# A recurrence spread over the projections of a hybrid decoder layer: later and held products, its end moved over the output projection, and norms regrouped

## The chip, the cores and the metric

The kernel runs on one core of a Trainium2 chip. A core has a matmul engine (TensorE, PE in the profile; PEld is its weight load), VectorE (DVE), ScalarE (ACT), GpSimd (POOL) and SyncE (SP), each with a queue of its own that it works off strictly in order, and 16 DMA engines that serve transfers asked for by SP's and POOL's queues. The metric is the device time of one launch in microseconds; the time of a kernel is the median of its runs.

## The reference

One layer of a decoder, on 512 prompt tokens and on 8 sampled sequences of 4 tokens. Everything is float32, width 2048.

```python
h = rms_norm(x, norm_mix_w)
proj = h @ w_in                      # [B_a|C_a|h_a|q|k|v|z: 1024 each | a: 8 | b: 8]
y_a = b_a * dwconv3(c_a * h_a)       # then RMSNorm over each group of 128
q, k, v = silu(dwconv4(q|k|v))       # q, k L2-normalised per head (8 heads of 128)
g = -exp(a_log) * softplus(a + dt_bias);  beta = sigmoid(b)
# gated delta rule, per head:
#   S_t = alpha_t S_{t-1} (I - beta_t k_t k_t^T) + beta_t v_t k_t^T ;  o_t = S_t q_t
o = rms_norm(o, dn_norm_w) * silu(z)
x = x + concat(y_a, o) @ w_out       # 2048 x 2048
h = rms_norm(x, norm_ffn_w)
x = x + square(relu(h @ w_up)) @ w_down     # 2048 -> 8192 -> 2048
return rms_norm(x, final_norm_w), new conv states, new S
```

The delta rule is evaluated in chunks: in each chunk a unit lower triangular system is inverted (here a substitution over 32 rows and then block products), and the state S passes from chunk to chunk.

## The kernel before

**Layout.** Activations lie transposed: 128 features on the partitions, tokens along the free axis. The 512 prompt tokens and 32 sampled ones make two halves of `HT` = 272 columns. A product of float32 accuracy is made of three products of rounded parts: `product` (L146) multiplies high weight by high activation, high by low, and low by high, for both halves, so one 128x128 block of weights costs six matmuls of 272 columns. `weight` loads up to 1024 columns of weights on SP's queue (L118) into one of two `w_raw` buffers, ScalarE rounds them (`w_hi`, L119), VectorE takes the rest (`w_lo`, L122); there are three buffers of each. `ahead` asks for weights two items early. `split` (L130, L131) does the same to an activation tile; 32 buffers of the pool `hl` hold the parts, all of them in use during the input projection.

**The mixer.** The input projection has 56 slabs of 128 output columns, in four groups (`gi`) of two heads: six slabs of q, k and v, six of the convolution path (C, h, B twice), two of z. The first three slabs of all run together while `x` arrives tile by tile; in that stretch ScalarE also squares the tiles and GpSimd and VectorE add them up (`ssq`), and the row norm follows (`rstd_rows`: products with ones at L153, then Ln and Exp on ScalarE at L156 and L157, then VectorE from L158). Each further slab has 16 blocks, 96 matmuls; after every second block the code calls `run_side`. I call the twelve matmuls between two calls a **share**; a slab is eight shares.

**Side work.** `run_side` advances a list of Python generators: `yield n` means "go on n shares later". Per group there are four kinds. `decays` loads and exponentiates the decay rows; it waits until the recurrence before is done. `delta` is the prompt's recurrence, appended after the sixth slab, so that 64 shares of its group are left: transposes and norms of k (L506), the in-chunk products (L532), a round trip through DRAM and the substitution of 31 steps on VectorE (L557, L561), another round trip (tiles `ti`, `tn`), transposes of v, then `yield W_SUBST`; then block products of 32x32 and 64x64 (L595, L607, L612, L618, L624), four chunks in which the state is passed on (L638, L644, L652, L662, L663), and the norm of the output per head (sums over features by L681, L682, then Ln and Exp at L685, L686), multiplied by `silu(z)` and written to the DRAM tile `cat`. `delta_sample` does the same for the sampled tokens (state products L738, four iterations L747, new states L782). `norm` closes a convolution slab (L472 to L479).

**Who sets the order.** Each engine's order is not the order of the code. A planner runs through the program with a cost model before the launch: it hands each engine, at each moment, the instruction of highest priority whose inputs it reckons ready. Priority is the place in the code, raised by `urgent` or `high_priority`. So an instruction whose inputs the planner reckons late is placed late, and everything behind it in its chain is then overdue and placed as soon as it is reckoned ready. On the chip that order is fixed, and an engine waits at an instruction whose input is really later. `keep_in_program_order` ties an instruction behind the one that stands before it in the code on its engine.

**After the mixer.** `run_side(True)` finishes what is left; then the sixteen tiles of `cat` are loaded and split (L866), the mixer's pools are closed, and tiles of new pools take the same memory, so their loads wait for the old tiles' last use: the residual `x2p` (eight tiles, L889, pool `g`), and later more. The output projection runs in two parts: first (`w_o1`) 16 output blocks over eight tiles of `cat`, added into `x2p` (L898), then (`w_o2`) the other eight, by halves, with squares for the second row norm. The up projection follows: three plain blocks, then `Pair`s that need seven block products instead of eight (`bilinear`, L1093) and load four quarter weights `w_q` each (L1043) and combine them on VectorE (L1053 to L1056), four tiles at a time in pool `g`. The down projection runs in visits of the same kind, from a new pool of six, with eight `Plain` items (L146, six us of products each) set between the first visits; it reads tiles `uc` back from DRAM. The last part adds the remaining terms, makes the third row norm and writes the output.

**Activation tables.** ScalarE needs a table that holds the function it is to compute. `ln_exp` loads one set that holds both Ln and Exp; where it isn't called, a load is placed before each function that the current set lacks (`ACT_TABLE_LOAD`, shown at the line of the function). The load at `ln_exp` has L79, that of Silu L84.

## Time and profile before

| | |
|---|---|
| Median of 3 runs | 2474.48 us (2472.3 to 2479.77) |
| The profiled execution's own time | 2472.83 us |
| Its span, first to last instruction | 2471.1 us |
| Mean granted TensorE clock | 0.986 |
| Instructions | 47391, of them 19089 matmuls |
| Moved by DMA | 398 MB, mean 161 GB/s |

The stages in the profiled execution: input projection from the first microseconds to 837, first part of the output projection to about 945, second part to about 1047, up projection to about 1740, down projection to about 2400, last part to 2455 on TensorE, and then row norm and output. In the profile's rows "a<-b,c" means that tile a is written from b and c, xN counts instructions, and a bracket at the end of a row gives the idle time of the engine before it and what ended it. Matmuls are pipelined and their ends are modelled, so starts are a better measure of TensorE's pace than busy time.

### The profile page before, as it was taken

The numbers are of one execution on the slowest core, as the hardware profiler recorded it, in microseconds if no ns is written. First come the engines' busy times: TensorE is split into PE (matmuls) and PEld (weight loads), VectorE is DVE, ScalarE is ACT, GpSimd is POOL, SyncE is SP. The second block draws the span as 40 slices with busy tenths as digits, with TensorE's granted clock in tenths as the row PEclk, the third lists the DMA queues.
The fourth block names the chain that finished last, engine by engine and source line by source line (L and its number), as shares of the span: only waits on it lengthen the run. The fifth ranks groups of instructions, "written<-read, shape, count | busy, mean of one in ns | idle before, by whom it ended". The sixth has DMA issues, their size and how long they took to land.

```text
span 2471.1 us, 47391 instructions
## 1 busy us (share of the span) xinstructions
PE 2407.6 (97%) x19089; PEld 2375.8 (96%) x19089; DVE 1803.2 (73%) x2939; ACT 1095.5 (44%) x1611; POOL 494.7 (20%) x776
## 2 busy tenths in 40 slices
PE   8999999999999999999999999999899999999997
PEld 7999999999999899898999999999899999999996
DVE  8776576567567635787888888888478877888885
ACT  5425334332531523565555555555233333333445
POOL 5124114213312303410111111101401212121003
PEclk9999999999998999999999999999999999999998
DMA  6233233332422535556555555556945656464433
GB/s 199 84 117 119 88 107 116 95 104 89 128 89 90 197 112 191 193 193 225 198 197 193 184 185 191 196 193 214 372 144 166 224 164 224 154 222 155 127 98 103
DMA packets 144276, 397.96 MB, mean 161 GB/s; under 512 B 35349, under 2 KB 44217, under 8 KB 144057
## 3 DMA queue, kind: packets, MB, share of 16 engines
q1 hardware_dynamic: 108648, 266.12, 34.2%
q0 software_dynamic: 35408, 128.82, 13.9%
q8 instruction: 150, 2.46, 0.4%
q14 instruction: 70, 0.57, 0.1%
HBM read 317.37 MB, written 77.49 MB: 160 GB/s over the span
## 4 chain that ended last, share of the span: by engine, by line
PE 80%; DVE 8%; DMA 7%; ACT 3%; issue 2%; SPq 0%; POOL 0%; DVEq 0%; ACTq 0%; POOLq 0%
PE ps_s L1093 45%; PE ps_big L146 27%; DVE w_lo L122 2%; PE ps_sm L146 2%; DMA w_raw<-in_w_up_dram 2%; DMA w_raw<-in_w_o_dram 2%; DMA w_q<-in_w_d_dram 2%; PE ps_s L146 1%; ACT w_hi L119 1%; DVE w_lo L1061 1%; PE ps_sm L738 1%; DVE x L937 0%; DVE x2v L1250 0%; PE ps_sm L532 0%; DMA tn<-ti 0%
## 5 line engine op out<-in xcount | busy, mean ns | idle before, releaser
L1060 ACT ACTIVATE w_hi<-w_q 128x768 fp32r<-128x768 f32 (+3 forms) x422 | 375.3, 889 | 554.5 <-PE ps_s L1093 461.4
L1093 PE MATMUL ps_s<-uc,w_hi 128*128 128x272 f32 x3136 | 594.6, 289 | 7.9 <-DVE x2v L898 3.9
L1093 PEld LDWEIGHTS ps_s<-uc,w_hi 128*128 128x128 f32 x3136 | 492.5, 189 | 11.7 <-ACT w_hi L1060 6.8
L1061 DVE TENSOR_TENSOR w_lo<-w_q,w_hi 128x768 fp32r<-128x768 f32 (+3 forms) x422 | 424.8, 1008 | 63.0 <-ACT w_hi L1060 61.4
L1093 PE MATMUL ps_s<-uc,w_lo 128*128 128x272 f32 x1568 | 451.5, 288 | 4.5 <-DVE w_lo L1061 4.5
L146 PE MATMUL ps_big<-x_hi,w_hi 128*128 128x272 f32 x1984 | 423.3, 293 | 1.5 <-ACT x_hi L134 1.5
L146 PE MATMUL ps_big<-x_hi,w_lo 128*128 128x272 f32 x1984 | 418.2, 291 | 2.6 <-DVE w_lo L122 2.6
L146 PE MATMUL ps_big<-x_lo,w_hi 128*128 128x272 f32 x1984 | 418.9, 292 | 0.3 <-DVE x_lo L137 0.3
L119 ACT ACTIVATE w_hi<-w_raw 128x1024 fp32r<-128x1024 f32 (+3 forms) x215 | 211.2, 982 | 406.0 <-PE ps_big L146 250.8
L122 DVE TENSOR_TENSOR w_lo<-w_raw,w_hi 128x1024 fp32r<-128x1024 f32 (+3 forms) x215 | 275.1, 1280 | 149.0 <-ACT w_hi L119 144.8
L146 PEld LDWEIGHTS ps_big<-x_hi,w_hi 128*128 128x128 f32 x1984 | 315.5, 189 | 5.4 <-ACT x_hi L134 2.2
L146 PEld LDWEIGHTS ps_big<-x_hi,w_lo 128*128 128x128 f32 x1984 | 314.5, 190 | 4.1 <-DVE w_lo L122 3.3
L146 PEld LDWEIGHTS ps_big<-x_lo,w_hi 128*128 128x128 f32 x1984 | 314.3, 190 | 1.0 <-DVE x_lo L137 0.5
L1093 PEld LDWEIGHTS ps_s<-uc,w_lo 128*128 128x128 f32 x1568 | 296.0, 189 | 4.9 <-DVE w_lo L1061 4.9
L1093 PE MATMUL ps_s<-c_hi,w_lo 128*128 128x272 f32 x928 | 267.7, 288 | 2.5 <-DVE w_lo L122 1.4
L1093 PE MATMUL ps_s<-c_hi,w_hi 128*128 128x272 f32 x928 | 266.5, 287 | 2.6 <-ACT w_hi L1060 2.2
L1093 PE MATMUL ps_s<-c_lo,w_hi 128*128 128x272 f32 x928 | 266.4, 287 | 0.0
L1160 POOL DMA_DIRECT2D uc<-ucd x196 | 106.5, 548 | 438.4 <-PE ps_s L1093 385.9
L898 DVE TENSOR_TENSOR x2v<-x2v,ps_s 128x272 f32<-128x272 f32 x326 | 139.8, 433 | 68.0 <-PE ps_s L1093 57.4
L1093 PEld LDWEIGHTS ps_s<-c_hi,w_lo 128*128 128x128 f32 x928 | 174.4, 188 | 3.5 <-DVE w_lo L122 1.8
L1093 PEld LDWEIGHTS ps_s<-c_hi,w_hi 128*128 128x128 f32 x928 | 174.6, 188 | 3.0 <-ACT w_hi L1060 2.4
L1093 PEld LDWEIGHTS ps_s<-c_lo,w_hi 128*128 128x128 f32 x928 | 174.4, 188 | 0.0
(378 smaller groups left out, 4304.5 us busy)
## 6 DMA issues: line engine op xcount, KB each, us to landing
w_q<-in_w_up_dram SPq DMA_DIRECT2D x116, 512.0 KB, 5.3
w_raw<-in_w_in_dram SPq DMA_DIRECT2D x106, 512.0 KB, 3.4
uc<-ucd POOLq DMA_DIRECT2D x196, 272.0 KB, 6.0
w_q<-in_w_d_dram SPq DMA_DIRECT2D x128, 384.0 KB, 3.3
w_raw<-in_w_o_dram SPq DMA_DIRECT2D x32, 512.0 KB, 3.5
ucd<-u_hi POOLq DMA_DIRECT2D x28, 544.0 KB, 5.7
ucd<-tc POOLq DMA_DIRECT2D x28, 544.0 KB, 6.9
w_raw<-in_w_up_dram SPq DMA_DIRECT2D x28, 512.0 KB, 3.6
```

The source lines that it names most:

```text
L119: S.activation(hi[:, c], raw[:, c], AF.Copy)
L122: V.tensor_tensor(lo[:, c], raw[:, c], hi[:, c].bitcast(F32), SUB)
L146: PE.matmul(ps[h], wp[:, c : c + P], x, start=start and i == 0, stop=stop and i == 2)
L738: PE.matmul(prq[rows, :], flat[:, 64 * b : 64 * b + 64], s0[:, b, :], start=b == 0, stop=b == NB - 1,)
L898: V.tensor_tensor(out, out, ps, ADD)
L1060: S.activation(hi, s, AF.Copy)
L1061: V.tensor_tensor(lo, s, hi.bitcast(F32), SUB)
L1093: PE.matmul(ps, wp[:, k * P : (k + 1) * P], xp, start=p in (1, 2, 5) and k == j == 0, stop=k == len(c) - 1 and j == 2, skip_group_check=True,)
L1160: nc.gpsimd.dma_start(t.bitcast(F32), uc_d[KS[j]][:, 2 * b : 2 * b + 2])
```

## The change

1. `W_SUBST` goes from 17 to 32, and three more `yield 1` stand between the halves of the block products; the sample path waits 13 shares instead of 2 before its iterations and 4 instead of 3 after them.
2. TensorE is called through a class `PE`: the first product or transpose of each side step is tied behind the product before it in the code.
3. After the last slab, twelve tiles of `cat` are loaded (four of them into a new pool `xe` of two buffers, early), the first two residual tiles take the same two buffers, and the first four blocks of the output projection run with `run_side` between them; only then is the side work drained and the rest of `cat` loaded. All sixteen blocks use the double accumulators.
4. The output norms of a group's two heads run side by side in tiles that reuse the recurrence's, with one table load; the products with `silu(z)` go to tiles of their own.
5. `ln_exp(True)` is called after the output projection's first part, ahead of the later row norms.
6. At the start, the last two tiles of `x` are squared before the last weights are asked for.
7. Pool `g` has six buffers instead of eight; each fourth tile of that kind comes from `xe`.
8. Five `Plain` items instead of three run before the first visit of the down projection, one (not two) after it, one (not two) after the second.

```diff
-W_SUBST = 17
+W_SUBST = 32
+N_MIX = 4
...
+    class PE:
+        step = False
+        @classmethod
+        def held(cls, ins):
+            if cls.step:
+                tc.keep_in_program_order(ins)
+                cls.step = False
+            return ins
+        @classmethod
+        def matmul(cls, *args, **kw):
+            return cls.held(nc.tensor.matmul(*args, **kw))
...
+    xep = pool("xe", 2)
...
+            if kp == KT // 2 - 1:
+                square_of(0)
+                square_of(1)
             w = weight(a["w_first"][kp], 2 * N_START * P, None if kp else first)
...
                 V.tensor_copy(x1[hi_], px[hi_])
+                yield 1
...
-            yield 2
+            yield 1
...
                 V.tensor_scalar(tt[lo_, :, hi_], py[lo_], -1.0, None, MUL)
+                if p2 == 0:
+                    yield 1
...
+            nk, nf = tile_in(dp, "nk", [P, 2, 2, L], tag="at"), tile_in(dp, "nf", [P, 2, L], F32R, tag="vs")
+            nl = tile_in(dp, "nl", [P, 2, L], F32R, tag="ke")
             for hl in range(2):
...
-                yield 5
-                pn = ps_small()
...
-                ln_exp(True)
...
+            yield 5
+            ln_exp(True)
+            for hl in range(2):
+                sk, pn = nk[:, 1, hl], ps_small()
+                PE.matmul(pn, ones_r, nf[:, hl], start=True, stop=False)
+                PE.matmul(pn, ones_r, nl[:, hl], start=False, stop=True)
...
+            while not z_done[gi]:
+                yield 3
+            for hl in range(2):
+                o = tmp()[:, :L].rearrange("p (a c) -> p a c", a=2)
+                G.tensor_tensor(o, og[:, hl, :, :HP], nk[:, 1, hl].rearrange("p (a c) -> p a c", a=2), MUL)
                 nc.gpsimd.dma_start(cat_d[8 + 2 * gi + hl][:, :, :HP], o)
...
-            yield 2
+            yield 13
             y = rq
...
-            yield 3
+            yield 4
...
                     try:
+                        PE.step = True
                         item[0] = next(item[1]) - 1
...
+            PE.step = False
...
+        cat = []
+        for n, i in enumerate(W_OUT_ORDER[:12]):
+            if n < 4:
+                if n % 2 == 0:
+                    pair = tile_in(xep, "cat2", [P, 2, 2, HT], tag="xe")
+                yr = pair[:, n % 2]
+            else:
+                yr = tmp2()
+            with tc.high_priority(offset=WPRIO if n < 4 else 0):
+                nc.sync.dma_start(yr, cat_d[i])
+            cat.append(split(yr, None))
+        x2p = [tile_in(xep, f"x2_{i}", [P, 2, 2, HT], tag="xe") for i in range(2)]
+        for i in range(2):
+            with urgent():
+                nc.sync.dma_start(x2p[i], a["x"][i])
...
+        def first_part(last, between):
+            for (ob, q), w in firsts:
+                if q == 0:
+                    first_part.ps = ps_big()
+                ps = first_part.ps
+                for k in range(N1 // 2):
+                    kk = N1 // 2 * q + k
+                    product(ps[0], w, k * P, cat[kk], kk == 0, kk == N1 - 1)
+                    if k % 2:
+                        between()
+                if q == 1:
+                    add(x2p[ob // 2][:, ob % 2], ps[1])
+                if (ob, q) == (last, 1):
+                    return
+
+        first_part(N_MIX - 1, run_side)
         run_side(True)
-        cat = []
-        for i in W_OUT_ORDER:
+        for i in W_OUT_ORDER[12:]:
             yr = tmp2()
             nc.sync.dma_start(yr, cat_d[i])
             cat.append(split(yr, None))
...
-    gp = pool("g", 8)
+    gp = pool("g", 6)
...
+    def gx_tile(i, name, shape):
+        return tile_in(xep, name, shape, tag="xe") if i % 4 == 3 else g_tile(name, shape)
...
-        if q == 0:
-            ps = ([ps_small(HT) for _ in range(2)], None) if ob in (2, 3) else ps_big()
...
+    first_part(KT - 1, lambda: None)
+    ln_exp(True)
...
-    items[0] = plains[:3] + items[0] + plains[3:5]
-    items[1] += plains[5:7]
+    items[0] = plains[:5] + items[0] + plains[5:6]
+    items[1] += plains[6:7]
     items[2] += plains[7:]
```

More of the change, by code (lines that the diff above doesn't have):

```diff
@@ L861, in trunk, with add @@
         assert next(jobs, None) is None
+        cat = []
[4 more added lines that the diff above has]
+                yr = pair[:, n % 2]
+            else:
+                yr = tmp2()
[4 more added lines that the diff above has]
+        for i in range(2):
+            with urgent():
+                nc.sync.dma_start(x2p[i], a["x"][i])
+        def add(out, ps):
+            with urgent():
+                V.tensor_tensor(out, out, ps, ADD)
+        firsts = ahead([(o, q) for o in range(KT) for q in range(2)],
+                       lambda it: weight(a["w_o1"][2 * it[0] + it[1]], N1 // 2 * P))
+        def first_part(last, between):
[13 more added lines that the diff above has]
+        first_part(N_MIX - 1, run_side)
         run_side(True)
-        cat = []
-        for i in W_OUT_ORDER:
+        for i in W_OUT_ORDER[12:]:
             yr = tmp2()
@@ L884, in c_tile @@
         return tile_in(p, name, [P, 2, HT], F32R, tag="hl" if p is hlp else "c")
-    x2p = [g_tile(f"x2_{i}", [P, 2, 2, HT]) for i in range(KT // 2)]
-    for i in range(KT // 2):
+    for i in range(2, KT // 2):
+        x2p.append(g_tile(f"x2_{i}", [P, 2, 2, HT]))
         with tc.high_priority(offset=WPRIO if i < 5 else 0):
@@ L894, in trunk @@
     uc_d = {m: tile_in(dram, f"ucd{m}", [P, 14, HT]) for m in range(N_PLAIN, NF - 1)}
-    def add(out, ps):
-        with urgent():
-            V.tensor_tensor(out, out, ps, ADD)
-    ps = None
-    for (ob, q), w in ahead([(o, q) for o in range(KT) for q in range(2)],
-                            lambda it: weight(a["w_o1"][2 * it[0] + it[1]], N1 // 2 * P)):
-        if q == 0:
-            ps = ([ps_small(HT) for _ in range(2)], None) if ob in (2, 3) else ps_big()
-        for k in range(N1 // 2):
-            kk = N1 // 2 * q + k
-            product(ps[0], w, k * P, cat[kk], kk == 0, kk == N1 - 1)
-        if q == 1 and ps[1] is not None:
-            add(x2[ob], ps[1])
-        elif q == 1:
-            for h in range(2):
-                add(x2[ob][:, h], ps[0][h])
+    first_part(KT - 1, lambda: None)
+    ln_exp(True)
     early.close()
@@ L1040, in load @@
                 with urgent():
-                    self.q = [self.tile(self.n) for _ in range(4)]
+                    self.q = [self.tile(self.n, i) for i in range(4)]
                     for t, s in zip(self.q, self.src):
@@ L1116, in residual @@
         for i in r:
[L1117 removed]
+            x2v.append(gx_tile(i, f"x2v{i}", [P, 2, 2, HT]))
             queue.dma_start(x2v[i], x2_d[i])
```

55 lines of the change are left out of this document (24 added, 31 removed).

## The prediction

> **What bounds the kernel now.** I read the page first: engine totals and the chain that ended last.
>
> ```profile
> span 2471.1 us, 47391 instructions
> PE 2407.6 (97%) x19089; PEld 2375.8 (96%) x19089; DVE 1803.2 (73%) x2939; ACT 1095.5 (44%) x1611; POOL 494.7 (20%) x776
> PE 80%; DVE 8%; DMA 7%; ACT 3%; issue 2%; SPq 0%; POOL 0%; DVEq 0%; ACTq 0%; POOLq 0%
> ```
>
> TensorE sets the time, so an edit is worth the TensorE time it gives back. A busy PE says little here, since a matmul that crawls at half clock also counts as busy. I therefore count matmul starts per stretch. Windows view: length, busy time with starts (x) of PE, PEld, DVE, ACT, POOL, then granted clock, DMA share, GB/s.
>
> ```profile
> 240.00:290.00 50.00, 50.00 (x401) 50.00 (x400) 28.76 (x37) 14.18 (x23) 13.20 (x30) 1.00 0.30 93
> 178.00:210.00 32.00, 30.70 (x304) 28.16 (x303) 21.87 (x66) 8.58 (x19) 11.00 (x12) 1.00 0.18 57
> 376.00:408.00 32.00, 30.10 (x276) 27.50 (x276) 19.39 (x61) 5.57 (x14) 6.86 (x8) 0.89 0.22 63
> 578.00:610.00 32.00, 30.86 (x283) 28.27 (x281) 19.71 (x61) 5.93 (x14) 6.92 (x9) 0.89 0.22 64
> 780.00:820.00 40.00, 38.11 (x309) 35.42 (x308) 23.38 (x66) 9.23 (x20) 10.58 (x12) 0.79 0.12 32
> 855.00:868.00 13.00, 8.47 (x52) 8.26 (x51) 4.13 (x7) 2.52 (x4) 0.00 (x0) 0.74 0.92 348
> 1760.00:1772.00 12.00, 4.79 (x23) 3.44 (x21) 4.79 (x14) 1.97 (x5) 6.66 (x13) 0.72 1.04 385
> 1055.00:1066.00 11.00, 9.00 (x59) 8.78 (x59) 8.26 (x16) 8.43 (x12) 0.36 (x1) 0.84 0.29 97
> 38.00:47.00 9.00, 5.96 (x32) 5.33 (x31) 7.00 (x13) 2.89 (x5) 0.41 (x1) 0.81 0.88 250
> 2429.00:2446.00 17.00, 16.03 (x122) 15.23 (x121) 12.20 (x21) 10.21 (x20) 6.18 (x7) 1.00 0.36 126
> ```
>
> The first row is the undisturbed pace: 401 starts in 50 us, **0.125 us** a 272-column product. By it the handover to the output projection (855 to 868) lost 13 - 52 x 0.125 = 6.5 us, the start of the down projection (1760 to 1772) 12 - 23 x 0.125 = 9.1, the second row norm (1055) 3.6, the first (38) 5.0, the one at 2429 1.8. The four recurrences (rows 2 to 5) need the small products priced apart. The same view of the slab products alone, then two stretches of group 3:
>
> ```profile
> 178.00:210.00 32.00, 18.75 (x109) 14.75 (x108) 1.00 0.18 57
> 376.00:408.00 32.00, 17.99 (x91) 13.93 (x90) 0.89 0.22 63
> 578.00:610.00 32.00, 18.22 (x95) 14.22 (x93) 0.89 0.22 64
> 780.00:820.00 40.00, 23.47 (x114) 18.97 (x113) 0.79 0.12 32
> 707.20:783.45 76.25, 68.25 (x524) 66.35 (x524) 1.00 0.36 109
> 783.45:816.10 32.65, 17.94 (x72) 13.77 (x72) 0.74 0.08 24
> ```
>
> And from the chain of waits (start, us, what) and PE's timeline, one row each for the price of a small product and for what starts a recurrence:
>
> ```profile
> 741.69 1.89 PE ps_sm L738 x16
> 778.59 4.21 DMA tn<-ti
> 789.55 1.90 PE ps_sm L618 x16
> ```
> ```profile
> 706.37 1.03 PE L506 MATMUL ps_sm<-ident,kq 128*128 128x128 f32 x8
> 783.49 0.69 PE L595 MATMUL ps_sm<-tn,at 32*32 32x32 f32 x16 [1.02 <-DVE tn L575]
> ```
>
> A full-size small product costs 1.89 / 16 = 0.118 us; a 64x64 one 0.119 at half clock, so 0.06; a 32x32 one 0.043. The code issues 80 of 32x32 and 32 of 64x64 per recurrence (eight products are sixteen instructions, as the L595 row shows). Group 3: 114 x 0.125 + 80 x 0.043 + 32 x 0.06 + 83 x 0.118 = 29.4 of 40 us, **lost 10.6**. Groups 0, 1, 2 the same way: 3.2, 6.7, 5.8. Sum 26.3 us. Granted clock explains 0.11 x 32 twice and 0.21 x 40, that is 15.4 of it.
>
> Why they lose is an order, visible in two counts. The code asks for L595 31 shares (of twelve products) after L506: 4 + 8 + 2 + 17. The trace has 524 / 12 = 43.7 shares between. So the planner found the substitution's answer (the tn transfer, row 778.59) later than asked; after that every step of the recurrence is overdue and goes out as soon as the planner believes it ready, with 72 slab products between L595 and 816 instead of the 19 shares (228) that its yields ask for. TensorE sees the whole chain of replies nearly bare.
>
> **The change, part by part.**
>
> *Substitution 17 to 32 shares, products held, three more yields.* L595 is now asked for 46 shares after L506, 2.3 shares (3.5 us) past where it stood; its wait was 1.02 us, so it finds its operand. Then 17 steps follow, each behind at least twelve products, 1.5 us. The reply that a step needs is a VectorE copy, at worst behind one weight split:
>
> ```profile
> 800.25 1.22 DVE L122 TENSOR_TENSOR w_lo<-w_raw,w_hi 128x1024 fp32r<-128x1024 f32 x1
> 801.38 0.48 DVE L646 COPY y<-ps_sm 128x128 f32<-128x128 f32 x2
> ```
>
> 1.7 us at worst, 0.48 at best, against 1.5 plus the step's own products (four at 0.118). Most steps are covered, and they now fall into the two z slabs, whose VectorE job is a single product. I take 22 of the 26.3 back; bounds 10 (0.25 us left on each of 68 steps) and 26. The held instruction blocks what is behind it on PE, slab products above all; that is what a wrong cover would cost, priced below. Recurrence and sample path now end five to seven shares into the next group's q slab, beside its decays and convolutions: VectorE stood at 28.76 of 50 us there, so I charge 1 us, 0 to 6.
>
> *Last group over four output blocks.* In the trace the handover loses like this (SP's queue, then PE's):
>
> ```profile
> 852.36 2.36 SPq L889 DMA_DIRECT2D x<-in_x_dram  x5
> 854.83 0.93 SPq L118 DMA_DIRECT2D w_raw<-in_w_o_dram  x2
> ```
> ```profile
> 863.26 0.82 PE L146 MATMUL ps_sm<-x_hi,w_hi 128*128 128x272 f32 x2 [4.53 <-ACT w_hi L119]
> ```
> ```profile
> x<-in_x_dram SPq DMA_DIRECT2D x8, 544.0 KB, 5.9
> w_raw<-in_w_o_dram SPq DMA_DIRECT2D x11, 256.0 KB, 3.3
> ```
>
> Five residual loads of 544 KB go out ahead of two weights, all in one burst; at 348 GB/s they take 8 us, and PE runs dry. After the change two residual tiles and four `cat` tiles have their own buffers and load earlier, and three urgent loads are left for the burst: about 5 us. But those wait for the mixer's memory, and the mixer now ends later: norms 10 shares (15 us) past the last slab, then ACT, VectorE and two POOL products, say 22 us. The fifth block needs its residual at 5 x 48 x 0.125 = 30 us and a second accumulator lends 6 more, so a 5.9 us load fits. Behind the waiting loads in SP's queue stand the `w_o1` weights, and TensorE waits for those. I take 4 of the 6.5; bounds -6 and 6.5.
>
> *One table for the norms.* ScalarE at the tail, and VectorE's two waits there (line, total, times, longest):
>
> ```profile
> 2455.49 1.28 ACT L156 ACT_TABLE_LOAD   x1
> 2456.79 0.49 ACT L156 ACTIVATE r<-ps_sm,eps_t 128x272 f32<-128x272 f32 x1
> 2457.30 1.28 ACT L157 ACT_TABLE_LOAD   x1
> 2458.59 0.43 ACT L157 ACTIVATE r<-r 128x272 f32<-128x272 f32 x1
> ```
> ```profile
> DVE rt L158 <- ACT r L157: 9.4, 2, 4.7
> ```
> ```profile
> DVE rt L158 <- ACT r L157: 5.2, 2, 2.6
> ```
>
> Both loads at the tail lie on the way to the end, nothing covers them: 2.56, less 0.3 for the result of the last row sum. At 999 and 1056 (last row) VectorE, which splits the weights, stands 2.6 us behind the same pair; freeing it gives about 3 of the 3.6 us lost at 1055 and 1 at 1000; 0.7 of the 1.8 at 2429. Term 7, bounds 3 (tail alone) and 10. It rests on Ln and Exp staying loaded through the Relus between, which no row shows. The Trainium skill (ScalarE: Activation LUTs, "Table sets: the hidden batching unit") lists relu and copy as filler of every set, which speaks for it. Its section "What ACT_TABLE_LOAD costs" puts a switch at about 2.66 us with a drain; here Ln starts 0.02 us after a 1.28 us load, so the trace disagrees; by the page the term would be about 14.
>
> *Plain products first.* The 9.1 us at 1760 (rows: who waits on SP, then the chain):
>
> ```profile
> SPq L1043 <- DMA ud<-u: 15.1, 1, 15.1
> ```
> ```profile
> 1756.33 11.12 DMA w_q<-in_w_d_dram
> ```
>
> The first quarter weights wait for memory of a tile on its way out, then 11.12 us in a saturated window (share 1.04), until 1767.5. Two more plain items are 2 x 48 x 0.125 = 12 us of work that needs none of this, and PE reaches the first visit at about 1773. Their two 512 KB weights go ahead (2.7 us at 385 GB/s), and later visits have one plain item less between them. Term 8, bounds 2 (a plain weight stuck behind the six waiting loads on SP) and 10.
>
> *Squares first at the start.* PE stood 5.0 us at 38 for the row sum, but VectorE has no gap before it; the same splits come 1.4 us later. Term 1, -1 to 4. *Six plus two g tiles*: the first quarters now wait for the fifth residual tile to be freed, not the fourth; -1, -3 to 0. *Row norms side by side, own output tiles, renamed tags*: the same ACT, VectorE and POOL operations on engines at 73% and below, nothing.
>
> **Sum**: 22 - 1 + 4 + 7 + 8 + 1 - 1 = 40 us. The profiled execution took 2472.8 (span 2471.1 plus 1.7), so 2432.8; it was 1.7 below the median of the runs, so **2434.5 us**.
>
> **The rivals.**
>
> *The clock stays low.* If the small products themselves pull the granted clock down, and not the bare replies between them, closing the waits doesn't bring it back and the 15.4 us stay: 40 - 15.4 = 24.6, so 2450. For it: the wait at L595 was only 1.02 us and the clock was 0.79 all the same. Against it: group 0, with the same products, kept 1.00. Chance 0.08. The Trainium skill (TensorE: Matmul & The Clock Gate, "HAM oscillation — how this bites in real kernels") ties the drop to gaps over about 3.4 us on TensorE; by that rule these short waits could not have caused it, and this rival would be the forecast, but the clock rows of groups 0 and 3 speak against the rule.
>
> *The handover gets worse.* If the mixer's memory comes 12 us later than I reckon, PE stands 12 us and 6.8 us at half clock, about 16 in place of a gain of 4: 2455. For it: SP's queue is in order and both loads share it. Chance 0.10.
>
> *It doesn't do what it says*: the planner still finds the substitution late and packs the steps. Then 22 is missing: 2457. Against it: 46 is over the 43.7 counted. Chance 0.08, half of it within no change.
>
> *Slower: held steps wait.* If the reply lags one convolution job more than the cover, 1.3 us on each of 68 steps is 88 us where 26.3 was: 62 worse, against 18 from the rest, so 2517. It decides from (18 + 26.3) / 68 = 0.65 us a step. Against it: the z slabs. Chance 0.06.
>
> **How the numbers follow.** Forecast 0.68, its own range 2417 to 2446. A change is told from none at 0.3%, 7.4 us. Faster 0.68 + 0.08 + 0.10 + 0.04 = 0.90, same 0.04, slower 0.06. The range takes in clock, handover and half of the third rival: 2417 to 2458.
>
> **What would show it.** L595 without a wait and 200 or more products until the end of its recurrence; granted clock 1.00 in all four; no table load after the output projection's first part; the first visit of the down projection without a wait of several us; five to seven shares of recurrence past the last slab. Wrong it is if PE rows at L644, L652 or L638 show waits near 1 us, or if SP waits for mixer tiles with weights behind.

## The result, and the profile after

| | before | after |
|---|---|---|
| Median of the runs beside each other | 2477.12 us (4 runs) | 2440.16 us (4 runs, 2438.37 to 2444.58) |
| The profiled execution's own time | 2472.83 us | 2444.58 us |
| Its span | 2471.1 us | 2442.8 us |
| Mean granted TensorE clock | 0.986 | 0.994 |

The ratio is 0.9854, with a 95% interval of 0.9827 to 0.988: faster by 1.5%, against the 2434.5 us forecast and inside the range of 2417 to 2458. The same kernel measured again on another chip gave 0.9881 (0.9857 to 0.9904), so 1.2 to 1.5% is what stands. The medians are 37.0 us apart here and 29.2 us on the other chip. The profiled execution of after is the slowest of its four, and that of before is 4.3 us faster than the median above; this pair differs by 28.3 us of span, and it is this pair that the stages below explain.

The page of after, its engine totals and the chain that ended last by engine:

```profile
span 2442.8 us, 47373 instructions
PE 2388.2 (98%) x19089; PEld 2362.3 (97%) x19089; DVE 1807.5 (74%) x2937; ACT 1080.9 (44%) x1598; POOL 495.8 (20%) x776
PE 83%; DVE 6%; DMA 6%; issue 2%; ACT 2%; SPq 0%; DVEq 0%; POOLq 0%; POOL 0%; ACTq 0%
```

TensorE has the same 19089 instructions and still sets the time. To see where the 28.3 us came from, I divided both executions at the same work: the 272-column products number 17832 in each, and the borders stand where TensorE has started 240, 5496, 5664, 7056, 7680, 12288, 13488 and 16512 of them and starts the next. The windows view of TensorE alone (stretch, length, PE busy with starts, granted clock, DMA share, GB/s), first of before:

```profile
0.00:46.82 46.82, 38.07 (x254) 0.96 0.69 214
46.82:852.50 805.68, 799.46 (x6487) 0.98 0.34 107
852.50:880.45 27.95, 23.43 (x171) 0.88 0.72 251
880.45:1066.39 185.94, 179.51 (x1398) 0.99 0.50 161
1066.39:1154.52 88.13, 81.76 (x626) 1.00 0.67 223
1154.52:1733.57 579.05, 577.93 (x4611) 1.00 0.56 197
1733.57:1898.45 164.88, 155.66 (x1200) 0.97 0.64 221
1898.45:2281.49 383.04, 380.79 (x3027) 1.00 0.58 191
2281.49:2471.10 189.61, 170.95 (x1334) 0.97 0.36 114
```

and of after:

```profile
0.00:43.33 43.33, 37.00 (x253) 1.00 0.64 207
43.33:837.81 794.48, 785.55 (x6486) 1.00 0.35 109
837.81:859.60 21.79, 21.75 (x169) 1.00 0.76 263
859.60:1039.54 179.94, 177.26 (x1399) 1.00 0.54 175
1039.54:1133.78 94.24, 84.62 (x626) 0.96 0.63 209
1133.78:1712.02 578.24, 577.47 (x4610) 1.00 0.56 197
1712.02:1876.16 164.14, 154.39 (x1201) 0.98 0.64 225
1876.16:2257.69 381.53, 380.20 (x3027) 1.00 0.58 191
2257.69:2442.80 185.11, 169.96 (x1334) 0.97 0.37 117
```

Row by row, after against before: start 3.5 us shorter; input projection with the recurrences, to ten shares into the output projection, 11.2; handover 6.2; rest of the output projection with the second row norm 6.0; plain up blocks and the start of the `Pair`s 6.1 **longer**; the other `Pair`s 0.8; start of the down projection 0.7; its rest 1.5; last part with the third norm and the tail 4.5. The sum is 28.3. So in this pair the recurrence gave half of what was forecast, the plain items next to nothing, and the start of the up projection took back more than allowed. How far such a row varies by itself is seen where one of the kernels further below runs the same code in a stage: the second stage with the recurrences of before took 811.7 us instead of 805.7 in the kernel with the table alone, and the start of the `Pair`s 91.0 us instead of 94.2 in the second execution of after. The second stage of after itself came out at 794.5 both times.

The stretches of after that answer to those shown of before (windows view as there: length, PE, PEld, DVE, ACT, POOL, clock, DMA share, GB/s): the last three recurrences, the handover, the start of the down projection, and one at 1112.

```profile
383.00:415.00 32.00, 30.53 (x282) 29.55 (x280) 17.59 (x47) 10.75 (x18) 5.94 (x9) 0.95 0.28 86
584.00:616.00 32.00, 30.52 (x280) 29.59 (x278) 17.40 (x47) 10.32 (x18) 5.95 (x9) 0.95 0.21 74
782.00:822.00 40.00, 38.15 (x362) 36.91 (x361) 29.30 (x73) 19.14 (x35) 10.10 (x14) 1.00 0.39 127
841.00:854.00 13.00, 12.96 (x101) 12.56 (x100) 5.58 (x7) 2.22 (x4) 4.43 (x4) 1.00 0.73 260
1738.00:1752.00 14.00, 7.54 (x48) 7.26 (x48) 4.25 (x10) 0.42 (x1) 8.46 (x16) 0.78 1.04 382
1112.00:1126.00 14.00, 9.33 (x52) 8.80 (x51) 11.38 (x12) 4.55 (x6) 0.00 (x0) 0.76 0.53 192
```

The last recurrence's clock went from 0.79 to 1.00, those of the middle two from 0.89 only to 0.95. The handover runs at full pace: 101 starts in 13 us, where 52 were. The start of the down projection still stands: 48 starts in 14 us. And at 1112, in the stage that got longer, there is a hole: 52 starts in 14 us. What TensorE waits for (waits view: total us, times, longest):

```profile
PE ps_s L76 <- DVE x2v L916: 10.8, 6, 6.5
PE ps_sm L76 <- DVE bo L193: 5.9, 4, 1.5
PE ps_s L76 <- ACT w_hi L1124: 4.9, 2, 4.2
```

All matmuls now have the line of the class `PE`, L76. These three waits are the places where the forecast failed, each in one timeline. **In each recurrence**, here in the last group (TensorE, then VectorE):

```profile
786.68 0.69 PE L76 MATMUL ps_sm<-tt,x 32*32 32x32 f32 x16
...
790.50 0.59 PE L76 MATMUL ps_sm<-tt,x 32*32 32x32 f32 x13 [1.44 <-DVE bo L193]
```
```profile
785.14 1.14 DVE L799 CAST yx<-y_s 32x128 fp32r<-32x128 f32 x1
788.07 0.15 DVE L188 TENSOR_SCALAR bo<-o 128x1 int32<-128x1 int32 x1
790.04 0.41 DVE L637 TENSOR_SCALAR tt<-ps_sm 32x256 f32<-32x256 f32 x1
```

The first half of the 32-row products `py` goes at 786.7. The second half goes into the same PSUM tile, so it waits until VectorE has read the first (L637); and VectorE first has to work, from 785.14 on, through six operations that round the sample path's results (L799 to L801) and nine of its short column operations (L787 and L188 to L194), which the sample's 13 shares of waiting put exactly there. The read comes at 790.04, the second half at 790.5.

**At the start of the down projection**, VectorE, then TensorE:

```profile
1747.71 0.43 DVE L1117 TENSOR_TENSOR w_s<-w_q 128x256 f32<-128x256 f32 x1 [16.63 <-DMA uc<-ucd]
```
```profile
1749.00 1.39 PE L76 MATMUL ps_s<-u,w_hi 128*128 128x272 f32 x4 [6.46 <-DVE x2v L916]
```

The first visit's weight sum (L1117) waits at the head of VectorE's queue, idle for 16.63 us, until its quarter weights land (the releaser named, `uc`, is one of the transfers that land with them). Behind it stand the adds of the plain items (L916), which alone free the PSUM banks of these items (the tiles `ps_s` that TensorE writes). The further plain items are there to cover the weights, and stop because of them.

**At the start of the `Pair`s**, VectorE, then TensorE:

```profile
1113.22 1.23 DVE L1117 TENSOR_TENSOR w_s<-w_q 128x1024 f32<-128x1024 f32 x1 [1.46 <-DMA w_q<-in_w_up_dram]
```
```profile
1118.33 0.59 PE L76 MATMUL ps_s<-c_hi,w_hi 128*128 128x272 f32 x1 [4.18 <-ACT w_hi L1124]
```

The tables did as told: between Ln and Exp of the third norm there is no load any more (ScalarE's timeline), and the last load of all is the one asked for behind the output projection's first part, at 911.9.

```profile
2429.81 0.49 ACT L179 ACTIVATE r<-ps_sm,eps_t 128x272 f32<-128x272 f32 x1 [0.26 <-PE ps_sm L76]
2430.33 0.43 ACT L180 ACTIVATE r<-r 128x272 f32<-128x272 f32 x1
```

### The profile page after: what moved, and what is told of

The parts are those of the page before. It is cut to its first block, busy times and chain, and to the rows that moved or that the text cites. A ratio compares the mean times of both kernels' runs of the same rounds, so it can differ in the third digit from the quotient of the medians.

```text
span 2442.8 us, 47373 instructions
## 1 busy us (share of the span) xinstructions
PE 2388.2 (98%) x19089; PEld 2362.3 (97%) x19089; DVE 1807.5 (74%) x2937; ACT 1080.9 (44%) x1598; POOL 495.8 (20%) x776
## 4 chain that ended last, share of the span: by engine, by line
PE 83%; DVE 6%; DMA 6%; issue 2%; ACT 2%; SPq 0%; DVEq 0%; POOLq 0%; POOL 0%; ACTq 0%
PE ps_s L76 46%; PE ps_big L76 29%; PE ps_sm L76 8%; DVE w_lo L145 2%; DMA w_raw<-in_w_o_dram 2%; DMA w_q<-in_w_d_dram 1%; DMA w_raw<-in_w_up_dram 1%; ACT w_hi L142 1%; DVE w_lo L1125 1%; DMA w_q<-in_w_up_dram 1%; DVE x L1001 0%; PE ps_sm L80 0%; DVE yx L799 0%; DMA w_raw<-in_w_d_dram 0%; DMA ud<-u 0%
## 5 line engine op out<-in xcount | busy, mean ns | idle before, releaser
L1124 ACT ACTIVATE w_hi<-w_q 128x768 fp32r<-128x768 f32 (+3 forms) x422 | 375.4, 890 | 555.7 <-PE ps_s L76 496.1
L76 PE MATMUL ps_s<-uc,w_hi 128*128 128x272 f32 x3136 | 592.1, 288 | 5.3 <-DVE x2v L916 4.4
L76 PEld LDWEIGHTS ps_s<-uc,w_hi 128*128 128x128 f32 x3136 | 491.0, 188 | 7.9 <-issue 5.3
L1125 DVE TENSOR_TENSOR w_lo<-w_q,w_hi 128x768 fp32r<-128x768 f32 (+3 forms) x422 | 425.5, 1009 | 59.5 <-ACT w_hi L1124 58.0
L76 PE MATMUL ps_s<-uc,w_lo 128*128 128x272 f32 x1568 | 450.3, 288 | 0.0
L76 PE MATMUL ps_big<-x_hi,w_hi 128*128 128x272 f32 x2016 | 426.4, 293 | 1.3 <-ACT x_hi L157 1.1
L76 PE MATMUL ps_big<-x_hi,w_lo 128*128 128x272 f32 x2016 | 419.3, 289 | 2.6 <-DVE w_lo L145 2.6
L76 PE MATMUL ps_big<-x_lo,w_hi 128*128 128x272 f32 x2016 | 420.2, 289 | 0.3 <-DVE x_lo L160 0.3
L76 PEld LDWEIGHTS ps_big<-x_hi,w_hi 128*128 128x128 f32 x2016 | 317.6, 189 | 5.8 <-ACT x_hi L157 2.3
L76 PEld LDWEIGHTS ps_big<-x_hi,w_lo 128*128 128x128 f32 x2016 | 316.4, 189 | 3.5 <-DVE w_lo L145 3.4
L76 PEld LDWEIGHTS ps_big<-x_lo,w_hi 128*128 128x128 f32 x2016 | 317.7, 189 | 0.7 <-DVE x_lo L160 0.5
L76 PEld LDWEIGHTS ps_s<-uc,w_lo 128*128 128x128 f32 x1568 | 295.0, 188 | 0.0
L76 PE MATMUL ps_s<-c_hi,w_hi 128*128 128x272 f32 x928 | 267.7, 288 | 4.8 <-ACT w_hi L1124 4.2
L76 PE MATMUL ps_s<-c_hi,w_lo 128*128 128x272 f32 x928 | 268.6, 289 | 1.2 <-DVE w_lo L145 0.7
L76 PE MATMUL ps_s<-c_lo,w_hi 128*128 128x272 f32 x928 | 267.6, 288 | 0.0
L916 DVE TENSOR_TENSOR x2v<-x2v,ps_s 128x272 f32<-128x272 f32 x326 | 140.2, 435 | 66.6 <-PE ps_s L76 64.6
L76 PEld LDWEIGHTS ps_s<-c_hi,w_hi 128*128 128x128 f32 x928 | 175.9, 189 | 5.3 <-ACT w_hi L1124 4.4
L76 PEld LDWEIGHTS ps_s<-c_hi,w_lo 128*128 128x128 f32 x928 | 175.5, 189 | 2.0 <-DVE w_lo L1125 1.0
L76 PEld LDWEIGHTS ps_s<-c_lo,w_hi 128*128 128x128 f32 x928 | 175.5, 189 | 0.0
```

The source lines that it names most:

```text
L76: return cls.held(nc.tensor.matmul(*args, **kw))
L916: V.tensor_tensor(out, out, ps, ADD)
L1124: S.activation(hi, s, AF.Copy)
L1125: V.tensor_tensor(lo, s, hi.bitcast(F32), SUB)
```

## The experiments

Each kernel was timed beside the kernel before on the same chip. "Stage" means the stretches between the borders above.

| run | median us | ratio to before, 95% | span of its profile |
|---|---|---|---|
| after without the pin | 2447.73 | 0.9893 (0.9869 to 0.9917) | 2448.3 |
| after, 17 shares | 2463.14 | 0.9952 (0.9932 to 0.9972) | 2462.5 |
| before with the table alone | 2467.25 | 0.9972 (0.9958 to 0.9987) | 2467.5 |
| after, weight sum behind the adds | 2437.29 | 0.9855 (0.9836 to 0.9873) | 2436.4 |
| after, plain items as before | 2444.55 | 0.9882 (0.9854 to 0.9911) | 2443.0 |
| after, quarters in other buffers | 2436.79 | 0.9853 (0.9823 to 0.9882) | 2434.3 |
| after, a PSUM tile per half | 2428.39 | 0.9821 (0.9791 to 0.9851) | 2424.5 |
| after, sample path waits 2 | 2439.36 | 0.9871 (0.9834 to 0.9908) | 2434.6 |
| after again | 2444.33 | 0.9881 (0.9857 to 0.9904) | 2440.1 |
| after, nothing mixed | 2459.85 | 0.9947 (0.9925 to 0.9969) | 2458.1 |
| after with three edits | 2420.64 | 0.9784 (0.9761 to 0.9807) | 2414.7 |
| the same, sixth plain item earlier | 2420.32 | 0.9787 (0.9766 to 0.9809) | 2418.6 |

Differences of 5 us lie inside these intervals, so where an edit acts in one place the stage of the trace decides. Letters A and B are the theories of the expectation that stands above each result.

### Is it the pin, or the later place?

```diff
         def held(cls, ins):
-            if cls.step:
-                tc.keep_in_program_order(ins)
-                cls.step = False
             return ins
```

> The changed kernel without the pin: TensorE's first instruction of each step of the recurrence is no longer kept behind the instruction before it in program order; the 32 shares of waiting, the single shares between the halves and the six-plus-two mix over the output projection stay. Theory A (the pin itself brings the recurrence's gain, about 10 us of the profiled pair's 28): the planner sets the small products by its own idea of when the triangular inverse comes back from memory, so they wait again: TensorE waits for VectorE's transpose of tn at L602 or for x at L624 appear in each group, the granted clock of the groups falls below full speed as before, and the time is 2447 to 2455 us (0.988 to 0.991 of before). Rival B (the later place in program order does it alone, the pin adds nothing): 2440 us within 3, no stretch at half clock beyond those of the changed kernel, and no wait for tn.

Measured: 2447.7 us, a place that A had named, but not by A's mechanism. The second stage takes 800.0 us; after has 794.5, before 805.7. Of the 11.2 us the pin thus carries about 5.5 and the later place in the code the rest, so B falls too. No wait for `tn` came back. What grew is the wait that after has at the second half of `py` (8.3 us in all in place of 5.9, with 3.4 us at half clock behind it in all four groups, where after had that in two).

The second kernel keeps the pin and asks for the first product 15 shares earlier:

```diff
-W_SUBST = 32
+W_SUBST = 17
```

> The changed kernel with 17 shares of waiting instead of 32, the pin kept. Theory A (a pinned step really waits where it stands): in the changed kernel tn is ready at 776.5 us and its first product runs at 779.8, some 2 shares of slack of 1.5 us each; 15 shares earlier is 23 us earlier, so each of the four groups waits some 20 us with the projection's products queued behind it: 60 to 80 us more, 2500 to 2520 us, with TensorE waits of 15 to 20 us on VectorE's transpose of tn and half clock after each. Rival B (the planner can still fill in front of the pinned product, as the pin ties it only to the one instruction before it): waits under 3 us a group, 2440 to 2455 us.

Measured: 2463.1 us, between the two theories and inside neither. The second stage takes 818.5 us, 24 more than after and 13 more than before. The waits view, then the windows view of the third group:

```profile
PE ps_sm L76 <- DVE tn L602: 5.7, 4, 2.4
```
```profile
585.00:602.50 17.50, 17.50 (x126) 16.25 (x127) 5.96 (x13) 1.72 (x3) 2.59 (x3) 0.51 0.07 21
```

The waits for `tn` are short, as B had it: the pin ties a step to one product only, and the planner puts others in front. The first 32-row product stands 43.7 shares behind the transposes of k in every group, as in before, though 31 are asked for; in after it stands at the 46.0 that are asked for. What costs is the clock: 17 us at half rate in three of the four groups, 8.5 us each, 25.6 us, with 126 starts in 17.5 us where full rate gives 140 even of the long products. That a pinned step asked for too early costs was right, the 15 to 20 us of bare waiting was not.

### The handover

The kernel runs out all side work where the mixing would begin:

```diff
+        run_side(True)
         cat = []
         for n, i in enumerate(W_OUT_ORDER[:12]):
```

> The changed kernel with all that is left of the recurrence run out behind the last slab, ahead of the first block of the output projection, so that nothing is mixed over its first four blocks; order of the cat loads, tables, plains and the rest unchanged. Theory A (the mixing gives what the trace showed at that place, a stall of 4.7 and 2.0 us gone): the stall comes back as bare small products with waits of 0.5 to 3 us near 820 to 860 us, 5 to 8 us more: 2445 to 2449 us. Rival B (what is left is so little that it hides behind the weight casts, and the stall went because the first cat tiles are loaded early): 2439 to 2442 us, no wait over 1 us near 840 us.

Measured: 2459.9 us, 15.5 more than after on the same chip, twice what A said and in A's place. TensorE's windows from the last steps of the recurrence on:

```profile
826.00:849.50 23.50, 15.18 (x53) 11.45 (x53) 11.35 (x17) 8.70 (x13) 10.21 (x10) 0.56 0.61 199
```

Stages two and three together take 831.3 us here, 816.3 in after and 833.6 in before. So the later, held steps alone gain almost nothing: they put off the bare replies to the end of the mixer, and only the mixing over the output projection lets them be covered. The two parts of the change are worth 17 us together and 2 us without the second, both against the one profiled execution of before. In after the first product of the output projection is the 5377th (56 slabs of 96 come before it), and the recurrence still runs ten shares, 120 products, beyond it (TensorE's timeline):

```profile
817.78 0.41 PE L76 MATMUL ps_big<-x_hi,w_hi 128*128 128x272 f32 x2
...
837.58 0.40 PE L76 MATMUL ps_sm<-nl,ones_r 128*128 128x512 f32 x1
```

### The table

```diff
+    ln_exp(True)
     early.close()
```

> The kernel before with one line of the change alone: the activation table for logarithm and exponential loaded once behind the first output part. Theory A (the table edit gives its whole term by itself): no table load after that place, the second norm's wait near 1055 us, the third's near 2430 us and the tail get shorter by 3 to 4, 0.7 and 2.3 us, together 7 to 9 us: 2468 to 2470 us (0.9964 to 0.9972 of before). Rival B (the loads were hidden for the most part; what the changed kernel gained there came from its side work being spread elsewhere): only the tail's 2.3 us, 2475 us (0.999).

Measured: 0.9972, 7 us (3 to 10 by the interval), as A said. The span of its profile is only 3.6 us shorter than that of before, because in this execution the recurrences, which are unchanged, took 6.0 us more, with 17.1 and 20.5 us at half clock in the second and third group. The windows view of this kernel, its rest of the output projection and the start of the `Pair`s:

```profile
886.65:1064.61 177.96, 176.68 (x1398) 1.00 0.52 169
1064.61:1156.26 91.65, 83.58 (x626) 0.98 0.64 215
```

The first is 8.0 us shorter than in before, more than the 4 of the forecast; the second 3.5 us longer: what TensorE gains at the second norm it partly waits for in the up blocks that follow (3.1 us for the first quarters' casts at 1141.8, where before had 2.2, and 3.4 us at half clock behind it). The last stage is 4.6 us shorter.

### The plain items

```diff
-    items[0] = plains[:5] + items[0] + plains[5:6]
-    items[1] += plains[6:7]
+    items[0] = plains[:3] + items[0] + plains[3:5]
+    items[1] += plains[5:7]
```

> The changed kernel with the eight plain items of the down projection laid out as in the kernel before: three ahead of the first visit, two behind it, two and one behind the next ones. Theory A (the two further plain items only exchanged one wait for another: the changed kernel waits 6.75 us at 1742 us for banks that VectorE has not read, the kernel before waited there for the casts of the first weights): the wait on the PSUM banks goes, waits on L1124 and L1125 of together 7 to 9 us come back near 1745 us, and the time is 2440 to 2443 us (0.985 to 0.9865 of before). Rival B (the prediction's step: five plain items ahead are worth 8 us): 2447 to 2449 us (0.988 to 0.989).

Measured: 2444.6 us; by its interval both theories stand, by the trace A: the stage takes 165.5 us against 164.1 in after, so the two further items are worth 1.4 us, not 8. The wait is at the first weights again (L1125, up to 4.1 us) in place of the PSUM banks.

The next kernel keeps the five items and holds the weight sum behind their adds:

```diff
-                    V.tensor_tensor(self.s1, a21, a22, ADD)
+                    s1 = V.tensor_tensor(self.s1, a21, a22, ADD)
+                    if isinstance(self.key, tuple) and self.key[0] == 0:
+                        tc.keep_in_program_order(s1)
```

> The changed kernel with one line more: the first visit's first weight sum (L1117) pinned on VectorE behind the last add of the five plain items. Theory A (VectorE's queue is what stalls the plain items: the sum waits for its weight quarters from 1731 to 1747.7 us with the adds that free the PSUM banks behind it): the TensorE wait of 6.75 us at 1742 us and the 6.8 us at half clock behind it go; a wait of 1 to 2 us may come at the visit's third product group, which has only 12 products ahead of it; 5 to 9 us less than the changed kernel: 2431 to 2435 us (0.9815 to 0.983 of before). Rival B (the stall moves: the weight sums come late and the visit waits for them as long): 2440 us, with a wait of 5 us or more on the weight casts (L1124, L1125) near 1752 us. Rival C (the wait has another cause, such as the loads of the residual or of the plain weights): the gap at 1742 us stays.

Measured: 0.9855, which alone shows nothing. In the trace the stage takes 158.6 us, 5.6 less than in after and 5.2 less than in its second execution, and the stretch that stood still there now runs through (windows view of this kernel):

```profile
1738.00:1752.00 14.00, 14.00 (x112) 14.00 (x112) 4.22 (x12) 0.84 (x2) 8.04 (x15) 1.00 1.04 384
```

112 starts in the 14 us where after had 48, at the same DMA share of 1.04. Theory A holds, and with it the reason: order in VectorE's queue, not a load. Its new wait of 1.5 us at the visit's third product group came too.

### The quarters

Both large buffers now serve the first pair, whose quarters then take the memory that is freed first:

```diff
-        return tile_in(xep, name, shape, tag="xe") if i % 4 == 3 else g_tile(name, shape)
+        return tile_in(xep, name, shape, tag="xe") if i % 8 in (2, 3) else g_tile(name, shape)
...
-    quad = lambda n, i: gx_tile(i, "w_q", [P, 1024])[:, :n]
+    quad = lambda m: lambda n, i: gx_tile(i + 4 * (m - N_PLAIN), "w_q", [P, 1024])[:, :n]
```

(The residual tiles count on in the same way.)

> The changed kernel with the two large buffers used otherwise: both hold quarters of the first pair of up blocks (and of every second pair), so that this pair's four quarters take the buffers of the first four column pairs of the residual, as in the kernel before; the number of buffers is unchanged. Theory A (the wait of 4.5 us at 1114 us and the 6.8 us at half clock at 1118 us come from the third quarter, whose load waits for the fifth column pair to be read): wait and half clock go, 5 to 8 us less than the changed kernel in the trace, 2433 to 2436 us. Rival B (VectorE is simply behind there with the casts of the combinations): TensorE still waits 3 us or more on L1124 or L1125 near 1114 us, 2439 to 2441 us.

Measured: 0.9853, which alone shows nothing either. The stage (windows view of this kernel):

```profile
1039.42:1126.40 86.98, 82.33 (x626) 1.00 0.68 221
```

7.3 us less than in after, 4.1 less than in its second execution, and without half clock; the wait of 4.2 us on L1124 is gone, which was 2.4 us or more in every kernel here that has the quarters as in after. Theory A. The stage before it took 2.3 us more than in after, so of the two stages together 5.0 us remain.

### The two halves of the 32-row step

```diff
-            px = ps_small(256).rearrange("p (u c) -> p u c", c=32)
             for p2 in (0, 64):
+                px = ps_small(256).rearrange("p (u c) -> p u c", c=32)
...
-            py = ps_small(256).rearrange("p (u c) -> p u c", c=32)
             for p2 in (0, 64):
+                py = ps_small(256).rearrange("p (u c) -> p u c", c=32)
```

> The changed kernel with a PSUM tile of its own for each of the two halves of the 32-row step (px and py), where both halves shared one. Theory A (the second half's products wait for VectorE to read the first half's result out of the same tile, and that reading stands behind the sample path's short column operations): the waits put down to bo at L193 (5.9 us, four times up to 1.5) and to x at L624 (1.6 us, four times) go, with them the stretches of 3.4 us at half clock at 391 and 592 us, 5 to 9 us less in the trace: 2431 to 2436 us. Rival B (the next step needs what VectorE writes anyway, so the wait goes to L644 or L650): 2438 to 2441 us, with four waits of 1 us or more elsewhere in the groups.

Measured: 2428.4 us, 0.9821: more than A said. The second stage, and the third group (windows view of this kernel; the first row is of TensorE alone):

```profile
42.70:825.99 783.29, 781.86 (x6487) 1.00 0.36 111
```
```profile
579.00:611.00 32.00, 32.00 (x303) 30.94 (x301) 18.92 (x48) 11.20 (x17) 6.79 (x11) 1.00 0.20 62
```

The stage takes 783.3 us, 11.2 less than after and 22.4 less than before. 303 starts in 32 us stand where before had 283, and the waits on L193 and L624 are gone in all groups. Only 7.5 us of the 11.2 are those waits; 3.4 more are the two stretches of 3.4 us at half clock behind them.

The other way to part the two is to leave the tiles and move the column operations back to where before had them:

```diff
-            yield 13
+            yield 2
             y = rq
```

> The changed kernel with the sample path's wait at its old 2 shares instead of 13, so that its short column operations run some 11 shares (17 us) ahead of the 32-row step. Theory A (it is the meeting of the column operations with the read-outs of the 32-row step that costs): the waits put down to bo at L193 go, without a change of the tiles; 3 to 8 us less than the changed kernel: 2432 to 2437 us. Rival B (earlier, the sample path meets VectorE's elimination of the triangular inverse, and tn comes later): waits for tn of 1 us or more in each group, 2440 to 2446 us.

Measured: 0.9871, not told apart from after. The wait on L193 went, and another of the same kind came, 11 shares earlier, TensorE's transpose waiting for the same column operations' result (waits view):

```profile
PE ps_sm L80 <- ACT on L789: 6.8, 4, 1.7
```

The second stage still came out 3.6 us shorter, since no group fell to half clock in this execution. So neither theory is shown: the column operations were what stood in the way, and moving them only moves the wait.

### Together

> The changed kernel itself once more, beside which the other three of this chip are read. Every theory expects 0.983 to 0.988 of before, 2436 to 2445 us. What it is to show is which of its waits recur: theory A (they come from the order of the queues) expects the gaps of 0.7 and 1.8 us on TensorE in each group, of about 4 us at 1114 us and of 6 to 7 us at 1742 us again, within half a microsecond; rival B (they were chance of one execution) expects at least one of the last two to be gone or halved.

Measured: 0.9881. All the waits recur within 0.6 us, a little more than A's half microsecond: 1.5 us in each group, 3.6 at the `Pair`s' start, 6.2 at the down projection's. Theory A. The half clock doesn't recur in the same way (last section).

> The changed kernel with three of the edits together: a PSUM tile for each half of the 32-row step, the quarters of the first pair in the buffers freed first, the first visit's first weight sum behind the last add of the plain items. Theory A (three separate places, so the gains seen in the traces add): 12 to 14 us in the groups, 5 to 7 us near 1114 us, 5 to 7 us near 1742 us, together 22 to 28 us less than the changed kernel: 2412 to 2418 us, 0.975 to 0.978 of before, and full granted clock in nearly all of the span up to 2400 us. Rival B (part of a gain is given back later, as the weight loads are the next bound): 2420 to 2427 us, with new waits on w_lo at L145 or on the weight quarters.

Measured: 2420.6 us against 2444.3 of after on the same chip, 23.7 less, and 0.9784 of before (0.9761 to 0.9807). The three edits add, as A had it for the difference; the time itself lies in B's range, since A reckoned from 2440. No wait on weights came that is longer than 1.5 us. The rows of the three stages:

```profile
42.58:825.91 783.33, 781.90 (x6486) 1.00 0.35 111
...
1027.60:1113.89 86.29, 82.03 (x626) 1.00 0.68 223
...
1693.55:1849.12 155.57, 152.52 (x1200) 1.00 0.66 236
```

11.2, 8.0 and 8.6 us less than in after, and from the 240th product to the last stage the granted clock is 1.00 throughout in this execution, the fastest of its five. This kernel beats both.

One more edit on top of the three:

```diff
-    items[0] = plains[:5] + items[0] + plains[5:6]
+    items[0] = plains[:5] + items[0][:2] + plains[5:6] + items[0][2:]
```

> As the kernel with the three edits, and the sixth plain item put between the second and the third product group of the first visit, ahead of the groups that need the weight sums. Theory A (the wait of 1.5 us on L1124 that the pin left there, for the sums and casts after the last add, is covered by that item's 6 us of products): 1 to 3 us less than the three edits, 2410 to 2417 us. Rival B (the visit's accumulation banks are held longer over it, and the next visit's items wait in turn): the same or up to 3 us more.

Measured: 2420.3 us, the same, as B allowed: TensorE waits 2.7 us once for a weight cast (L1126) at 1749 us instead.

## Why the prediction was right or wrong

The verdict and the range were right. The sum of 40 us was too high by 12 in the profiled pair (by 3 and 11 in the two pairs of medians), and that it came out this close is in part luck: errors of both signs met.

| term | forecast | measured in the stages |
|---|---|---|
| recurrence, with collisions | 22 - 1 | 11.2 |
| handover | 4 (-6 to 6.5) | 6.2 |
| tables | 7 (3 to 10) | 6.0 + 4.5, with some 3.5 given back behind it; alone 7 |
| plain items | 8 (2 to 10) | 0.7 |
| start | 1 (-1 to 4) | 3.5 |
| g tiles | -1 (-3 to 0) | -6.1 |
| the rest | 0 | 0.8 + 1.5 |

**Recurrence: a term mis-sized.** The count of its loss is borne out: with the halves' tiles apart the stage gains 22.4 us, where 22 were forecast. What failed is "the reply that a step needs is a VectorE copy, at worst behind one weight split". For the second half of `px` and `py` the wait is not for the step's own operand but for the reading of the first half, which shares the tile; and ahead of the reading of `py` stood fifteen small operations of the sample path, not one split. The new `yield 1` between the halves covers 1.5 us, but the reading began 2.7 us after the first half's end (787.37 to 790.04). I had looked at each step's operands and not at what else the product overwrites or lies beside, and the sample path's moved shares I had booked as a flat 1 us.

**Plain items: the step failed.** "Two more plain items are 2 x 48 x 0.125 = 12 us of work that needs none of this" is wrong: their products need none of it, their adds stand on VectorE behind an instruction that does. The kernel with the sum pinned behind the adds shows it: its stage is 6.3 us shorter than that of before, and with all three edits 9.3, around the 8 forecast.

**The g tiles: a term mis-sized.** The mechanism, quarters that wait for the fifth residual tile, is shown by the kernel with the buffers exchanged (7.3 us). The forecast put it at 1 us, 3 at most. It didn't reckon that three sums on VectorE (1.2 us each, from the L1117 at 1113.22 on) and a cast on ScalarE (1.06 us) follow the third quarter before TensorE has weights again at 1118.33, nor the 6.8 us at half clock behind a wait of 4.2 us. Not all of the 6.1 us is the quarters': with the table alone, and the quarters as in before, the stage also came out 3.5 us longer, and the second execution of after had 2.9 instead of 6.1.

**Handover and tables: right, on the good side.** No stall was left at the handover; the rival of late mixer memory didn't come. How much of that the early `cat` and residual tiles do was not tried apart. SP did wait 4.8 us for a mixer tile with weights behind it (a residual load at 845.1), one of the signs of being wrong, but TensorE waited for nothing there. That the term can't be read by itself was missed: without the mixing the loss there would have been 15 us, not the 6.5 counted in before, since the held steps push their chain into it. Of the tables, Ln and Exp stayed loaded through the Relus between, as assumed. The 1.28 us load without a further 1.4 us of drain held as well: alone the edit gave 7 us (3 to 10). The estimate of about 14 from the figure in the Trainium skill (ScalarE: Activation LUTs, "What ACT_TABLE_LOAD costs") lies outside that.

**Start: mis-sized.** The 5.0 us at 38 were not all given back by the splits that come later: TensorE reaches the 240th product 3.5 us earlier. Which of the moved squares does it was not tried.

**The rivals.** "The clock stays low" falls: in the kernel with separate tiles the same small products run at clock 1.00 in all groups. "It doesn't do what it says" falls with the starts into `ps_big`, the products of the slabs and then of the output projection, from the second half of the first 32-row products of the last group to the last product of its norm (windows view of after): 292, where 200 were asked for. The first half ran at 779.83 without a wait.

```profile
783.63:837.60 53.97, 40.98 (x292) 1.00 0.38 122
```

"Held steps wait" fell as a whole; with 17 shares a pinned product does wait, but 2.4 us at most. The waits named as signs of being wrong (near 1 us at L644, L652, L638) stayed away, with at most 0.5 us there; the waits came at a place that the list hadn't. Two of the signs of being right didn't come: full clock in all four groups, and a start of the down projection without a wait of several us.

## What to carry to other kernels

Before work is moved to cover a wait, look at what every engine that it uses has queued at that place: products are no cover while the adds that free their banks stand behind an instruction that waits for the same load. Where two halves of a small product take turns, give each its own PSUM tile, or the second waits for the first to be read, by whatever else that reader has to do. And price a wait on TensorE with the half clock that may follow it: in the profile of after 6.8 us at half rate, 3.4 us lost, stand behind the waits of 4.2 and of 6.5 us, and 3.4 us, 1.7 lost, behind two of the four waits of 1.5.

## What the runs showed of the hardware

The granted clock has two values here, 1.00 and 0.50, and the stretches at half rate are about 3.4 us or a multiple of it (6.8, 17.1, 20.5), but for the one that each kernel ends in. They can follow waits that are far shorter than 3.4 us, but don't always: after the same wait of 1.47 and 1.48 us at the second half of `py`, the second group fell to half and the first did not (windows view of after):

```profile
390.90:394.30 3.40, 3.40 (x17) 3.40 (x16) 1.59 (x2) 1.91 (x3) 0.00 (x0) 0.50 0.21 52
...
187.00:200.00 13.00, 11.52 (x129) 10.85 (x126) 7.88 (x24) 5.04 (x7) 2.35 (x5) 1.00 0.19 64
```

In the second execution of the same kernel it was the second and the fourth group, where it had been the second and the third. Over the six executions here that have this wait in every group, 10 of the 24 groups fell. Without the pin, where the wait is 2.1 us, four of four did. With the sample path at 2 shares, waits of 1.7 us at another place of each group had none behind them in four of four. That alone is a few us between executions that are otherwise alike. The Trainium skill (TensorE: Matmul & The Clock Gate, "What's actually happening") says that the chip watches a window of about 3.4 us that runs freely, so that a result depends on where in it the work falls; the lengths and the chance here agree with that. The rule of the Trainium skill against idle gaps of over about 3.4 us ("HAM oscillation — how this bites in real kernels") does not describe these: the longest wait ahead of the stretch at 390.9 was 1.5 us. What decides when a short wait counts stays open. With the three edits two gaps of 1.8 and 1.7 us between starts were left ahead of the last stage (at 1734 and 1784), and the clock did not fall behind them. With the sixth plain item moved it fell at 1040.5 behind waits of only 1.1 and 0.7 us, and at 1750.4 behind one of 2.7.
